# FFN blocks 4 to 10 with five steps by seven products, 9 of 27 sets of weight sums formed by VectorE, and a transpose in halves

## The chip, the cores and the metric

One of the cores of a Trainium2 chip runs one program. The metric is the device time of one execution in microseconds (us), as the median of several runs. A profile belongs to one execution of its own: its span goes from the first to the last instruction, and that execution's time is a little longer than the span.

Names used below: PE is the matrix engine (TensorE), DVE the vector engine, ACT the scalar engine, POOL is GpSimd, SP is the engine that issues most of the DMAs. SBUF is the on-chip memory, PSUM the accumulators of PE. Each engine takes its instructions strictly in program order, and an instruction that waits holds up everything behind it on that engine.

## The reference, cut to what matters

The program computes one decoder layer for 256 positions and a model width of 2048. The change touches the feed-forward network and the preparation of its weights:

```python
a = rmsnorm(h, norm_ffn_pre[layer])
gt, up = jnp.split(a @ w_ffn_gate_up[layer], [D_FF], axis=-1)    # D_FF = 5632
ff = (jax.nn.silu(gt) * up) @ w_ffn_down[layer]
h = h + rmsnorm(ff, norm_ffn_post[layer])
```

Ahead of it stand the big projection of the input (`a @ w_in`, 17408 columns), attention in three dilated groups, a gated recurrence, two branch projections and the mixing projection. Everything is float32, and the kernel keeps that precision by splitting.

## The kernel before

**Splitting.** Each float32 operand is split into a high part (rounded to the type that PE multiplies) and a low part (what is left). ACT writes the high part and DVE subtracts it from the original for the low part. A product is then three matmuls: high by high, high by low, low by high.

**Steps.** The weights are streamed once. A *step* takes 256 rows of a weight matrix by 1024 columns (two groups of 512), 1 MB, into one of three `raw` tiles of SBUF. ACT writes the high part `w` (three tiles, line 441 or 434), DVE the low part `wl` (line 456 or 436), and PE multiplies both with the 256 positions. In blocks: 2 halves of the rows, 2 halves of the columns, 2 halves of the positions give 8 block products and thus 24 matmuls of 128x128 by 512 columns. A *step by seven* does the same with 7 block products, after Strassen and Winograd, thus 21 matmuls. It needs four sums of the activation's blocks (`h7[m]`, made once for each pair of rows m by `pair_sums`) and four sums of the weight's blocks. Of these, one takes the place of the first quarter of `raw`, three stand in a tile `sum` of 1536 columns, which is split too: high part `dh` (ACT, line 454), low part `dl` (DVE, line 458). `dh` and `dl` share four tiles, that is two steps.

**Where the weight sums come from.** The list of a block's steps, for instance `GATE_UP4`, holds pairs (m, s). With s = 0 the step is plain. With s = 1 DVE forms the sums when the step is split (three additions, lines 445 to 451). With s = 2 they lie ready in device memory as `presum`, formed long before, and `fetch_sums` brings 768 KB of them to SBUF and `load_wide` the remaining quarter. The step's ordinary load is unchanged in size.

**Forming `presum`.** `weight_sums` is a generator of GpSimd DMAs that copy and add up within device memory, 8 DMAs of 256 KB for each set. `ahead_of_time(i)` advances it once at the end of an item, after a tiny copy on POOL (line 344, `beats`) that waits until the load three items ahead has landed. Before, there are 20 sets, two for each of the FFN blocks 1 to 10.

**Items.** The program is one list of items, worked off by a loop at the end of the kernel. Items 0 to 79 are ten blocks of eight steps of the big projection; 80 to 175 are its query and key columns in smaller *chunks*; 176 to 191 are gate columns; 192 to 207 the recurrence's branch, 208 to 223 the attention's branch (four blocks of four chunks, each chunk 12 matmuls); 224 to 239 the mixing; then come eleven FFN blocks of eight steps, and 44 steps of the down projection. Attention and recurrence run as generators (`lanes`), advanced once an item.

At item i the code first splits item i + 2 (`split`: a high part on ACT, a low part on DVE, and by seven also `dh` and `dl`), then issues the DMAs of `fetch_sums` for item i + 4 and of the load that is three raw tiles ahead, then multiplies item i, then advances what finishes earlier blocks, then `ahead_of_time`. That is the order on every engine. Since there are three `w` tiles, the high part of item i + 2 can be written only when PE has done with item i - 1.

**Finishing an FFN block.** `evac_ffn` adds up the four accumulators with DVE (line 537) and applies silu with ACT (line 1461); a product (line 1463), two casts (line 1414), four DMA transposes issued by SP (line 1420), two more casts (line 1429) and a store issued by ACT (line 1431) turn the result for the down projection. All of it happens during the first half of the next block.

**Memory phases.** At item 210 (`make_room`, called with c = 2 in the first block of the attention's branch) the tiles of the attention phase are closed.

**Planes.** `turned_inputs` brings gate and query inputs of the recurrence back from device memory with four DMA transposes (`planes`) in items 72 to 75.

Of the kernel before, what the change touches and what calls it, by code (L numbers as in the profile page):

```python
# [43 lines left out]
]  # L44
GATE_UP3 = [(3, 0), (4, 0), (0, 2), (5, 0), (1, 1), (6, 0), (2, 2), (7, 0)]
GATE_UP4 = [(4, 0), (5, 0), (0, 2), (6, 0), (1, 1), (2, 2), (3, 1), (7, 0)]
DOWN = [[(m, m in by7) for m in range(KF // 2)] for by7 in (range(4, 20, 3), (2, 4, 7, 10, 13, 16, 18))]

SPARSE = 128
N_F, N_RAW, N_SPLIT, AHEAD, WARM, BRIDGE = 17, 3, 3, 2, 8, 6  # L50


# [49 lines left out]
def tile_hybrid_block(ctx: ExitStack, tc: tile.TileContext, t, out):  # L102
# [194 lines left out]
    def weight_sums(jobs):  # L297
# [25 lines left out]
        for at in range(len(jobs) + 3):  # L323
# [5 lines left out]
            yield  # L329
            yield  # L330

    def fetch_sums(i):
        if i < len(items) and items[i][0] is steps:
            n = items[i][1]
            if n in pre:
                pre_in[n] = sum_slot()
                nc.sync.dma_start(pre_in[n], pre[n][:, 512:])

    def ahead_of_time(i):

        kind, n = items[i][:2]
        if back and (kind is steps or n >= SPARSE or n % 3):
            ahead = items[i + 3][0][items[i + 3][1]][2]
            nc.gpsimd.tensor_copy(beats, ahead[:, 1023:1024])  # L344
            advance(back)
# [213 lines left out]
    def pair_sums(src, out, slot, pairs=H7):  # L559

        for m in pairs:
            f = ptile("f").rearrange("p (k t) -> p k t", k=2)
            x = src.slots[m]
            nc.vector.tensor_add(f, x[:, :, 0, :].bitcast(F32), x[:, :, 1, :].bitcast(F32))
            dst = slot().rearrange("p (z n t) -> p z n t", z=2, n=4)
            yield
            for part in seven_sums(f, dst):
                yield
                part()
            out[m] = sums_of(dst)  # L570
            yield
# [95 lines left out]
        return row[:, None, :].to_broadcast([P, n, S])  # L667

    evacs, turns, lanes, queue = deque(), deque(), [deque(), deque()], deque()
    back, turned, hold, gathers = deque(), deque(), [False], []  # L670
    ready = set()

    def advance(q):
# [7 lines left out]
    def flush(q):  # L681
        while q:
            advance(q)
# [111 lines left out]
    def turned_inputs():  # L795

        planes = {}
        for half, name in product(range(2), "fq"):
            planes[name, half] = rslot("planes").bitcast(U16)
            nc.sync.dma_start_transpose(  # L800
                planes[name, half].rearrange("p (n t) -> p n t", n=8), waits[name, half]
            )
            yield
        nc.sync.dma_start(lmask, t["lmask"])

        def join(copy, name, half, z):
# [569 lines left out]
    def more_h(c):  # L1376
        if c + 1 < KD // 2:
            transpose_in(h_t, colg[:, 16:32], hT[0], c + 1)
        if c == 3:
            mix_gain(3, 1, wides[last_mix])  # L1380
            residual_of(6, (0, 1), False)
            residual_of(7, (0, 1), False)
            lanes[0].append(second_norm())
        if c == 4:
            lanes[1].append(pair_sums(hT[0], h7, lambda: rslot("so"), range(4)))

    def second_norm():
        ss, s2 = small("ss"), small("s2")
# [202 lines left out]
    def make_room(c):  # L1591
        if c == 2:
            flush(evacs)
            end_phase1()

    early = [
# [47 lines left out]
    add_wide_block(w, (0, FF), PLAIN, lambda k: hT[0](k), None, evac_first, True, mid=more_h)  # L1644
    spare = wides[-1], 0
    for j in range(1, 11):
        add_wide_block(w, (512 * j, FF + 512 * j), GATE_UP4 if j > 1 else GATE_UP3, lambda k: hT[0](k),
                       lambda m: h7[m], evac_ffn, j % 2 == 0,
                       pre=begin_wides if j == 1 else None, turn=1)
    for j in range(2):  # L1650
# [3 lines left out]

    wides[len(early) - 1].pre = lambda: turned.append(turned_inputs())
    wides[-3].post = lambda c: fetch_act(c // 2) if c in (1, 3) else None
    back.append(
        weight_sums([n for n, (b, i, *_) in enumerate(steps) if b.order[i][1] == 2])
    )

    load_x(0, 0, 256)
    load_wide(0, ((0, (0,)), (0, (1,))))
# [111 lines left out]
```

## Time and profile before

| what | value |
|---|---|
| runs of the kernel before | 1681.19, 1682.56 and 1685.92 us, median 1682.56 us |
| the profiled execution | 1683.17 us; its span is 1681.3 us, so 1.87 us lie around the span |
| DVE in the FFN blocks, busy in each 50 us from 1100 to 1400 us | 43.4 to 45.3 us |
| DMA in the same stretch | busy 0.85 to 0.95, 261 to 290 GB/s |
| DVE from 650 to 850 us | 26.5 to 33.3 us of each 50 us |
| DMA queues over the whole span | 423.47 MB, a mean of 252 GB/s |

How to read the page: the first row says how long each engine was busy. A PE that is busy all the time need not be at its peak, because a matmul's end is modelled, so the distance between the starts of matmuls is the better measure. The chain of work that ended last says which engine's work fills the span. The timeline shows start, duration and, in square brackets, how long the engine had been idle and what ended the wait. A busy engine costs nothing as long as PE does not wait for it.

### The profile page before, as it was taken

The numbers are of one execution on the slowest core, as the hardware profiler recorded it, in microseconds if no ns is written. First come the engines' busy times: TensorE is split into PE (matmuls) and PEld (weight loads), VectorE is DVE, ScalarE is ACT, GpSimd is POOL, SyncE is SP. The second block draws the span as 40 slices with busy tenths as digits, with TensorE's granted clock in tenths as the row PEclk, the third lists the DMA queues.
The fourth block names the chain that finished last, engine by engine and source line by source line (L and its number), as shares of the span: only waits on it lengthen the run. The fifth ranks groups of instructions, "written<-read, shape, count | busy, mean of one in ns | idle before, by whom it ended". The sixth has DMA issues, their size and how long they took to land.

```text
span 1681.3 us, 21780 instructions
## 1 busy us (share of the span) xinstructions
PE 1668.5 (99%) x8023; PEld 1397.5 (83%) x8023; DVE 1374.6 (82%) x1433; ACT 1001.3 (60%) x1077; POOL 238.0 (14%) x358
## 2 busy tenths in 40 slices
PE   9999999999999999999999999999999999999997
PEld 7888888888888888888888888888888888888886
DVE  6988888888796786674568978899888888998987
ACT  6667555555555555555545547666666666665653
POOL 0012333232352221222230100000000000000000
PEclk9999999999999999999999999999999999999999
DMA  8678999999988887778899746999888989987773
GB/s 279 216 250 263 288 275 279 276 284 261 280 232 236 256 232 184 195 226 265 254 222 308 227 173 201 283 275 289 268 267 273 271 271 277 274 282 261 240 266 114
DMA packets 258284, 423.47 MB, mean 252 GB/s; under 512 B 46801, under 2 KB 97153, under 8 KB 258177
## 3 DMA queue, kind: packets, MB, share of 16 engines
q1 hardware_dynamic: 231728, 360.83, 67.5%
q0 software_dynamic: 17984, 41.97, 12.5%
q10 hardware_dynamic: 8464, 19.28, 3.4%
q8 instruction: 63, 1.03, 0.3%
q14 instruction: 45, 0.36, 0.1%
HBM read 397.89 MB, written 58.20 MB: 271 GB/s over the span
## 4 chain that ended last, share of the span: by engine, by line
PE 98%; DVE 1%; ACT 1%; issue 0%; DVEq 0%; ACTq 0%
PE acc L139 59%; PE aux L139 37%; PE aux L991 0%; PE aux L632 0%; DVE fz L1552 0%; DVE wl L436 0%; ACT junk L1506 0%; PE aux L619 0%; DVE e L537 0%; DVE w L382 0%; ACT w L381 0%; ACT w L434 0%; PE aux L1187 0%; PE aux L1294 0%; DVE yT L600 0%
## 5 line engine op out<-in xcount | busy, mean ns | idle before, releaser
L436 DVE TENSOR_TENSOR wl<-raw,w 128x2048 fp32r<-128x2048 f32 (+1 forms) x150 | 327.3, 2189 | 79.9 <-ACT w L434 77.7
L434 ACT ACTIVATE w<-raw 128x2048 fp32r<-128x2048 f32 (+1 forms) x150 | 273.7, 1833 | 120.3 <-PE aux L139 33.8
L382 DVE TENSOR_TENSOR w<-raw,w 128x1024 fp32r<-128x1024 f32 x144 | 176.4, 1225 | 129.4 <-ACT w L381 129.3
L139 PE MATMUL acc<-xT,w 128*128 128x512 f32 (+1 forms) x1536 | 275.6, 338 | 0.0
L139 PEld LDWEIGHTS acc<-xT,w 128*128 128x128 f32 x1536 | 233.9, 188 | 33.9 <-DVE w L382 0.7
L381 ACT ACTIVATE w<-raw 128x1024 fp32r<-128x1024 f32 x144 | 152.0, 1058 | 153.4 <-PE acc L139 114.3
L344 POOL COPY beats<-raw 128x1 f32<-128x1 f32 x185 | 129.7, 701 | 746.1 <-DMA raw<-in_w_in 563.4
L456 DVE TENSOR_TENSOR wl<-raw,w 128x2048 fp32r<-128x2048 f32 x83 | 190.1, 2290 | 32.0 <-ACT w L441 16.5
L139 PE MATMUL acc<-w,xT 128*128 128x512 f32 x694 | 207.1, 391 | 0.0
L139 PE MATMUL acc<-w,hT 128*128 128x512 f32 x510 | 166.7, 391 | 0.4 <-DVE hT L1306 0.4
L444 ACT ACTIVATE w<-raw 128x1536 fp32r<-128x1536 f32 x63 | 93.9, 1491 | 111.1 <-PE acc L139 33.9
L139 PEld LDWEIGHTS acc<-w,xT 128*128 128x128 f32 x694 | 129.9, 188 | 26.8
L458 DVE TENSOR_TENSOR dl<-sum,dh 128x1536 fp32r<-128x1536 f32 x83 | 145.5, 1753 | 3.0 <-ACT dh L454 3.0
L139 PE MATMUL aux<-w,xT 128*128 128x512 f32 x454 | 145.0, 389 | 0.0
L139 PE MATMUL aux<-w,hT 128*128 128x512 f32 x414 | 134.6, 389 | 0.0
L454 ACT ACTIVATE dh<-sum 128x1536 fp32r<-128x1536 f32 x83 | 123.3, 1485 | 12.2 <-PE aux L139 4.1
L139 PEld LDWEIGHTS acc<-w,hT 128*128 128x128 f32 x510 | 95.7, 188 | 20.5 <-DVE hT L1306 0.9
L139 PEld LDWEIGHTS aux<-w,xT 128*128 128x128 f32 x454 | 85.2, 188 | 17.7
L139 PE MATMUL acc<-wl,hT 128*128 128x512 f32 x255 | 99.2, 389 | 0.0
L139 PE MATMUL acc<-wl,xT 128*128 128x512 f32 x251 | 97.7, 389 | 0.0
L139 PEld LDWEIGHTS aux<-w,hT 128*128 128x128 f32 x414 | 77.7, 188 | 16.1
L139 PE MATMUL aux<-w,a 128*128 128x512 f32 x282 | 89.1, 389 | 0.0
(282 smaller groups left out, 3032.8 us busy)
## 6 DMA issues: line engine op xcount, KB each, us to landing
raw<-in_w_in SPq DMA_DIRECT2D x270, 512.0 KB, 6.1
raw<-in_w_ffn_gate_up SPq DMA_DIRECT2D x156, 512.0 KB, 5.4
raw<-in_w_ffn_down SPq DMA_DIRECT2D x88, 512.0 KB, 5.6
presum<-in_w_ffn_gate_up POOLq DMA_DIRECT2D x120, 256.0 KB, 6.5
raw<-in_w_mix_out SPq DMA_DIRECT2D x32, 512.0 KB, 5.1
sum<-presum SPq DMA_DIRECT2D x20, 768.0 KB, 6.7
act<-acts SPq DMA_DIRECT2D x22, 512.0 KB, 6.8
presum<-presum POOLq DMA_DIRECT2D x40, 256.0 KB, 6.4
```

The lines of the kernel that those rows point to most:

```text
L139: nc.tensor.matmul(ps, lhsT, rhs, start=start, stop=stop, skip_group_check=True)
L344: nc.gpsimd.tensor_copy(beats, ahead[:, 1023:1024])
L381: nc.scalar.activation(wh, raw, AF.Copy)
L382: nc.vector.tensor_sub(wl, raw, wh.bitcast(F32))
L434: nc.scalar.activation(hi[:, c], raw[:, c], AF.Copy)
L436: nc.vector.tensor_sub(lo[:, c], raw[:, c], hi[:, c].bitcast(F32))
L444: nc.scalar.activation(hi[:, 512:], raw[:, 512:], AF.Copy)
L454: nc.scalar.activation(high, sums, AF.Copy)
L456: nc.vector.tensor_sub(lo, raw, hi.bitcast(F32))
L458: nc.vector.tensor_sub(low, sums, high.bitcast(F32))
```

## The change

- **Five steps by seven.** A new list `GATE_UP5` is used for FFN blocks 4 to 10 in place of `GATE_UP4`. Position for position the kinds of steps are the same but at the fourth place of eight, where a plain step becomes one with s = 2. Block 1 keeps `GATE_UP3`, blocks 2 and 3 keep `GATE_UP4`. For the fifth pair of rows `pair_sums` makes `h7[4]`, after a pause of eight advances.
- **27 sets.** Blocks 1 to 3 have two sets each, blocks 4 to 10 three. 18 of them (blocks 1 to 6 and 10) come from `weight_sums` as before.
- **Nine sets by DVE.** Those of blocks 7 to 9 are made by a new generator, `weight_sums_beside`: SP loads four quarters of 256 KB into two tiles, three items later DVE adds (two additions, then one and one in the next items), one item later ACT issues two stores of 512 KB. One such set takes nine items. Two of these generators run from items 166 and 181 on, and `make_room` runs what is left of them to its end at item 210.
- **Pacing of `weight_sums`.** Up to chunk 95 it now advances in seven items of eight (before: two of three), from chunk 96 to 137 not at all, and not in wide block 9 (items 72 to 79).
- **Planes in halves.** Eight DMA transposes of half the size, one an item, in place of four.

```diff
--- before.py
+++ after.py
@@ -44,9 +44,10 @@
 ]
 GATE_UP3 = [(3, 0), (4, 0), (0, 2), (5, 0), (1, 1), (6, 0), (2, 2), (7, 0)]
 GATE_UP4 = [(4, 0), (5, 0), (0, 2), (6, 0), (1, 1), (2, 2), (3, 1), (7, 0)]
+GATE_UP5 = [(5, 0), (6, 0), (0, 2), (2, 2), (1, 1), (4, 2), (3, 1), (7, 0)]
 DOWN = [[(m, m in by7) for m in range(KF // 2)] for by7 in (range(4, 20, 3), (2, 4, 7, 10, 13, 16, 18))]
 
-SPARSE = 128
+PAUSE, QUIET, BESIDE = (96, 138), 9, (166, 181)
 N_F, N_RAW, N_SPLIT, AHEAD, WARM, BRIDGE = 17, 3, 3, 2, 8, 6
 
 
@@ -329,6 +330,28 @@
             yield
             yield
 
+    def weight_sums_beside(jobs):
+
+        for n in jobs:
+            x = [fslot("pre") for _ in range(2)]
+            b, i = steps[n][:2]
+            m = b.order[i][0]
+            r = [x[g][:, c * 512 : (c + 1) * 512] for g, c in ((0, 1), (0, 0), (1, 0), (1, 1))]
+            for q, (g, k) in enumerate(product(range(2), repeat=2)):
+                rows = slice((2 * m + k) * P, (2 * m + k + 1) * P)
+                nc.sync.dma_start(r[q], b.w[rows, b.cols[g] : b.cols[g] + 512])
+            for _ in range(3):
+                yield
+            for to, by in ((2, 0), (0, 1), (1, 2), (3, 1)):
+                nc.vector.tensor_add(r[to], r[to], r[by])
+                if by:
+                    yield
+            pre[n] = dram.tile([P, 2048], F32, name=nm("presum"))
+            for g in range(2):
+                nc.scalar.dma_start(pre[n][:, g * 1024 : (g + 1) * 1024], x[g])
+            for _ in range(3):
+                yield
+
     def fetch_sums(i):
         if i < len(items) and items[i][0] is steps:
             n = items[i][1]
@@ -338,8 +361,15 @@
 
     def ahead_of_time(i):
 
+        for n, q in enumerate(beside):
+            if i >= BESIDE[n]:
+                advance(q)
         kind, n = items[i][:2]
-        if back and (kind is steps or n >= SPARSE or n % 3):
+        if kind is chunks:
+            parts = n % 8 > 0 if n < PAUSE[0] else n >= PAUSE[1]
+        else:
+            parts = n // 8 != QUIET
+        if back and parts:
             ahead = items[i + 3][0][items[i + 3][1]][2]
             nc.gpsimd.tensor_copy(beats, ahead[:, 1023:1024])
             advance(back)
@@ -559,6 +589,8 @@
     def pair_sums(src, out, slot, pairs=H7):
 
         for m in pairs:
+            for _ in range(8 if m == 4 else 0):
+                yield
             f = ptile("f").rearrange("p (k t) -> p k t", k=2)
             x = src.slots[m]
             nc.vector.tensor_add(f, x[:, :, 0, :].bitcast(F32), x[:, :, 1, :].bitcast(F32))
@@ -667,7 +699,7 @@
         return row[:, None, :].to_broadcast([P, n, S])
 
     evacs, turns, lanes, queue = deque(), deque(), [deque(), deque()], deque()
-    back, turned, hold, gathers = deque(), deque(), [False], []
+    back, beside, turned, hold, gathers = deque(), (deque(), deque()), deque(), [False], []
     ready = set()
 
     def advance(q):
@@ -797,10 +829,13 @@
         planes = {}
         for half, name in product(range(2), "fq"):
             planes[name, half] = rslot("planes").bitcast(U16)
-            nc.sync.dma_start_transpose(
-                planes[name, half].rearrange("p (n t) -> p n t", n=8), waits[name, half]
-            )
-            yield
+            for z in range(2):
+                c = slice(z * 512, (z + 1) * 512)
+                nc.sync.dma_start_transpose(
+                    planes[name, half][:, z * 1024 : (z + 1) * 1024].rearrange("p (n t) -> p n t", n=4),
+                    waits[name, half][:, c],
+                )
+                yield
         nc.sync.dma_start(lmask, t["lmask"])
 
         def join(copy, name, half, z):
@@ -1382,7 +1417,7 @@
             residual_of(7, (0, 1), False)
             lanes[0].append(second_norm())
         if c == 4:
-            lanes[1].append(pair_sums(hT[0], h7, lambda: rslot("so"), range(4)))
+            lanes[1].append(pair_sums(hT[0], h7, lambda: rslot("so"), range(5)))
 
     def second_norm():
         ss, s2 = small("ss"), small("s2")
@@ -1591,6 +1626,8 @@
     def make_room(c):
         if c == 2:
             flush(evacs)
+            for q in beside:
+                flush(q)
             end_phase1()
 
     early = [
@@ -1644,7 +1681,7 @@
     add_wide_block(w, (0, FF), PLAIN, lambda k: hT[0](k), None, evac_first, True, mid=more_h)
     spare = wides[-1], 0
     for j in range(1, 11):
-        add_wide_block(w, (512 * j, FF + 512 * j), GATE_UP4 if j > 1 else GATE_UP3, lambda k: hT[0](k),
+        add_wide_block(w, (512 * j, FF + 512 * j), (None, GATE_UP3, GATE_UP4, GATE_UP4)[j] if j < 4 else GATE_UP5, lambda k: hT[0](k),
                        lambda m: h7[m], evac_ffn, j % 2 == 0,
                        pre=begin_wides if j == 1 else None, turn=1)
     for j in range(2):
@@ -1654,9 +1691,10 @@
 
     wides[len(early) - 1].pre = lambda: turned.append(turned_inputs())
     wides[-3].post = lambda c: fetch_act(c // 2) if c in (1, 3) else None
-    back.append(
-        weight_sums([n for n, (b, i, *_) in enumerate(steps) if b.order[i][1] == 2])
-    )
+    kept = [n for n, (b, i, *_) in enumerate(steps) if b.order[i][1] == 2]
+    back.append(weight_sums(kept[:15] + kept[24:]))
+    for n, q in enumerate(beside):
+        q.append(weight_sums_beside(kept[15:24][5 * n : 5 * n + 5]))
 
     load_x(0, 0, 256)
     load_wide(0, ((0, (0,)), (0, (1,))))
```

Two places show how the instructions move. The first is on DVE in an FFN block from the fourth on: the low part of the third step (`wl`, `dl`), the product that finishes the block before (`e`), and the next two or three steps. Before:

```order
L456 TENSOR_TENSOR wl_10188<-raw_10090,w_10187 128x2048
L458 TENSOR_TENSOR dl_10191<-sum_10119,dh_10190 128x1536
L1463 TENSOR_TENSOR e_10136<-e_10136 128x1024
L436 TENSOR_TENSOR wl_10229<-raw_10121,w_10228 128x2048
L445 TENSOR_TENSOR sum_10269<-raw_10154 128x1024
L450 TENSOR_TENSOR raw_10154<-raw_10154,sum_10269 128x512
```

The same place of the changed kernel, whose lines in the file have moved down by 30 to 35:

```order
L486 TENSOR_TENSOR wl_10296<-raw_10195,w_10295 128x2048
L488 TENSOR_TENSOR dl_10299<-sum_10224,dh_10298 128x1536
L1498 TENSOR_TENSOR e_10242<-e_10242 128x1024
L486 TENSOR_TENSOR wl_10337<-raw_10226,w_10336 128x2048
L488 TENSOR_TENSOR dl_10340<-sum_10260,dh_10339 128x1536
L475 TENSOR_TENSOR sum_10381<-raw_10262 128x1024
L480 TENSOR_TENSOR raw_10262<-raw_10262,sum_10381 128x512
```

One `dl` has come in; on ACT one `dh` comes in at the same place, and on SP two more DMAs (the quarter of `presum` and 768 KB of `sum`). Nothing else moves in these blocks.

The second place is item 210, where `make_room` ends the two new generators. On SP, loads of the attention's branch (`raw`) and the four quarters of the ninth set (`pre`) stand like this in the changed kernel:

```order
L272 DMA raw_7253<-in_w_attn_branch 128x2x512 x2
L272 DMA raw_7292<-in_w_attn_branch 128x2x512 x2
L342 DMA pre_7314<-in_w_ffn_gate_up 128x512 x2
L342 DMA pre_7315<-in_w_ffn_gate_up 128x512 x2
L272 DMA raw_7339<-in_w_attn_branch 128x2x512 x2
```

The load `raw_7292` takes the tile of `raw_7145`, whose last reader is the low part `w_7320` of item 211. On DVE, the low parts of items 210 to 214 (`w`), before:

```order
L382 TENSOR_TENSOR w_7203<-raw_7069,w_7203 128x1024
L1214 TENSOR_TENSOR part_7223<-acc_7122,gate_6846 128x512
L382 TENSOR_TENSOR w_7227<-raw_7069,w_7227 128x1024
L1214 TENSOR_TENSOR part_7223<-acc_7123,gate_6846 128x512
L382 TENSOR_TENSOR w_7245<-raw_7119,w_7245 128x1024
L382 TENSOR_TENSOR w_7270<-raw_7119,w_7270 128x1024
L382 TENSOR_TENSOR w_7289<-raw_7167,w_7289 128x1024
```

and in the changed kernel:

```order
L412 TENSOR_TENSOR w_7320<-raw_7145,w_7320 128x1024
L1249 TENSOR_TENSOR part_7309<-acc_7205,gate_6916 128x512
L412 TENSOR_TENSOR w_7336<-raw_7201,w_7336 128x1024
L346 TENSOR_TENSOR pre_7315<-pre_7315,pre_7314 128x512
L346 TENSOR_TENSOR pre_7314<-pre_7314 128x512
L346 TENSOR_TENSOR pre_7314<-pre_7314,pre_7315 128x512
L346 TENSOR_TENSOR pre_7315<-pre_7315,pre_7314 128x512
L412 TENSOR_TENSOR w_7366<-raw_7201,w_7366 128x1024
```

The four additions of the last set stand directly between the low parts of items 212 and 213, one low part behind the one that frees the tile for `raw_7292`. On ACT the two stores of that set stand between the high parts of items 212 and 213:

```order
L411 ACTIVATE w_7336<-raw_7201 128x1024
L351 DMA presum_7358<-pre_7314 128x1024
L351 DMA presum_7358<-pre_7315 128x1024
L411 ACTIVATE w_7366<-raw_7201 128x1024
L411 ACTIVATE w_7381<-raw_7253 128x1024
```

The eight other sets have their additions spread over three items, and their stores stand one item behind the last addition.

## The prediction

> **What bounds the kernel now.** I read the page first, then the waits of PE, the chain of waits, and then one FFN block on each engine.
>
> ```profile
> span 1681.3 us, 21780 instructions
> ...
> PE 1668.5 (99%) x8023; PEld 1397.5 (83%) x8023; DVE 1374.6 (82%) x1433; ACT 1001.3 (60%) x1077; POOL 238.0 (14%) x358
> ...
> PE 98%; DVE 1%; ACT 1%; issue 0%; DVEq 0%; ACTq 0%
> ```
>
> PE fills the span and the chain. Since a busy PE need not be at its peak, I look at whom it waited for, and at how fast its matmuls follow each other.
>
> ```profile
> PE aux L632 <- DVE wl L392: 1.3, 1, 1.3
> PE aux L139 <- DVE warm L163: 1.2, 1, 1.2
> PE acc L139 <- DVE hT L1306: 0.4, 1, 0.4
> PE acc L139 <- DVE gate L1224: 0.2, 1, 0.2
> PE aux L991 <- DVE p L985: 0.2, 1, 0.2
> ```
>
> Those are all waits of PE in the whole execution: 2.5 us at the start and 0.8 us later. So nothing that only removes waits can win even a microsecond; a gain must come from fewer matmuls.
>
> ```profile
> 1196.49 11.56 PE aux L139 x51
> ...
> 1237.29 11.56 PE acc L139 x51
> 1252.25 6.80 PE acc L139 x30
> ```
>
> In the chain, 51 matmuls take 11.56 us and 30 take 6.80 us: 0.2267 us each. The same place of the next FFN block comes 40.80 us later, which is 180 matmuls (4 plain steps of 24, 4 by seven of 21) at 0.2267 us, without a gap. A plain step takes 5.44 us, one by seven 4.76 us.
>
> **The change part by part.** *Matmuls.* In blocks 4 to 10 one plain step becomes one by seven: 7 x 3 = 21 matmuls less, 21 x 0.2267 = **-4.76 us**. A block then takes 177 x 0.2267 = 40.12 us, if DVE, ACT and the DMAs keep up.
>
> *DVE in these blocks.* Each gets one more `dl`.
>
> ```profile
> 1196.55:1237.35 40.80, 40.80 (x181) 33.78 (x180) 36.06 (x27) 27.23 (x22) 0.00 (x0) 1.00 0.87 268
> ```
>
> ```profile
> 1213.33 2.29 DVE L456 TENSOR_TENSOR wl<-raw,w 128x2048 fp32r<-128x2048 f32 x1
> 1215.53 1.75 DVE L458 TENSOR_TENSOR dl<-sum,dh 128x1536 fp32r<-128x1536 f32 x1
> 1217.20 1.22 DVE L445 TENSOR_TENSOR sum<-raw 128x1024 f32<-128x1024 f32 x1
> 1218.45 0.69 DVE L450 TENSOR_TENSOR raw<-raw,sum 128x512 f32<-128x512 f32 x1
> 1219.18 0.69 DVE L451 TENSOR_TENSOR sum<-raw 128x512 f32<-128x512 f32 x1
> ...
> 1234.85 1.88 DVE L537 TENSOR_TENSOR e<-aux,e 128x512 f32<-128x512 f32 x3
> 1237.33 0.69 DVE L537 TENSOR_TENSOR e<-aux,e 128x512 f32<-128x512 f32 x1 [0.60 <-PE aux L139]
> 1239.33 2.29 DVE L456 TENSOR_TENSOR wl<-raw,w 128x2048 fp32r<-128x2048 f32 x1 [1.31 <-ACT w L441]
> ```
>
> DVE is busy for 36.06 us of a block and idle for 4.74. With 1.75 us for `dl` it needs 37.8 of 40.12 us, so at most 2.3 us of waiting may be left. Which waits stay when DVE runs late? Those for PE go, since PE is then ahead. One stays: after the third L537 ends at 1236.73, ACT has still to do a silu and the next high part before DVE can start the `wl` of 1239.33; these 2.60 us hold only one more L537 of 0.69, so 1.9 us are idle whatever the lag. 37.8 + 1.9 = 39.7 us against 40.12: it fits, by 0.4 us. I cost DVE at nothing here, with little cover; its price without cover is a rival below.
>
> *ACT in these blocks.* One more `dh` of 1.49 us, in a queue that is busy for 27.2 of 40.8 us.
>
> ```profile
> 1215.18 2.60 ACT L1429 ACTIVATE act<-e 128x1024 uint16<-128x1024 uint16 x2 [1.20 <-DMA e<-e]
> 1217.81 0.33 ACTq L1431 DMA_DIRECT2D acts<-act  x1
> 1218.24 1.49 ACT L444 ACTIVATE w<-raw 128x1536 fp32r<-128x1536 f32 x1 [0.46 <-ACT act L1429]
> 1219.63 0.61 ACT L452 ACTIVATE w<-raw 128x512 fp32r<-128x512 f32 x1
> 1222.14 1.49 ACT L454 ACTIVATE dh<-sum 128x1536 fp32r<-128x1536 f32 x1 [1.90 <-PE aux L139]
> ```
>
> The last row shows a `dh` that waits for PE to leave the step that last used its tile. With five steps by seven in a row this wait comes earlier: the sixth step's `dh` waits for the fourth step's end, 2 x 5.44 + 2 x 4.76 = 20.40 us into the block. Behind it on ACT stand the casts, the store and the seventh step's high part, and behind that DVE's `wl`: 1.49 + 2.60 + 0.33 + 1.49 + 0.61 + 2.29 = 8.8 us, so 29.2. PE wants that low part in the second matmul of the seventh step, at 20.40 + 2 x 4.76 + 0.23 = 30.15. So **1.0 us of slack** remains at the tightest place. The casts wait for four transposes; behind a `dh` of 1.49 us they start at about 18.6 + 1.5 = 20.1 us into the block (18.63 is 1215.18 less 1196.55), before 21.9, when that `dh` ends, so they stay hidden.
>
> *DMAs in these blocks.* 768 KB more in each.
>
> ```profile
> sum<-presum SPq DMA_DIRECT2D x20, 768.0 KB, 6.7
> ...
> 1230.00:1240.00 10.00, 10.00 (x46) 8.28 (x45) 7.89 (x9) 5.73 (x5) 0.00 (x0) 1.00 0.99 360
> ```
>
> 268 GB/s over 40.8 us are 10.9 MB; with 0.79 MB more in 40.12 us it is 292 GB/s, while a busy 10 us moves 360. A sum is issued some 10 us before its `dh` and lands in 6.7. Nothing, with a rival for the other case.
>
> *The nine sets of DVE.* 36 additions of 0.69 us (L450's shape) are 25 us, 18 stores at 0.33 us (L1431) are 6 us of ACT.
>
> ```profile
> 690.00:912.00 222.00, 221.62 (x1155) 188.28 (x1154) 144.36 (x208) 117.56 (x154) 51.16 (x93) 1.00 0.85 241
> ```
>
> There DVE idles for 78 us and ACT for 104. For eight sets the additions come two or three items behind the loads' issue; an item of 3.6 us or so makes that 7 to 11 us, and a late one delays low parts with two items of room. Between 0 and 2 us; I take 0.3, near the row.
>
> *The ninth set* is the exception. Item 210 ends it at once.
>
> ```profile
> 856.01 1.23 DVE L382 TENSOR_TENSOR w<-raw,w 128x1024 fp32r<-128x1024 f32 x1 [0.89 <-ACT w L381]
> ...
> 858.73 1.23 DVE L382 TENSOR_TENSOR w<-raw,w 128x1024 fp32r<-128x1024 f32 x1 [0.89 <-ACT w L381]
> ...
> 865.80 1.07 ACT L381 ACTIVATE w<-raw 128x1024 fp32r<-128x1024 f32 x1 [1.66 <-PE acc L139]
> ...
> 1200.85 0.34 SPq L284 DMA_DIRECT2D raw<-presum  x1
> ...
> 1206.29 0.89 SPq L290 DMA_DIRECT2D raw<-in_w_ffn_gate_up  x2
> ...
> raw<-in_w_ffn_gate_up SPq DMA_DIRECT2D x20, 256.0 KB, 4.4
> ...
> presum<-in_w_ffn_gate_up POOLq DMA_DIRECT2D x120, 256.0 KB, 6.5
> ...
> DMA to landing us min/median/max: 3.0/5.6/9.3
> ```
>
> Item 211's low part (the row at 856.01; in the order, the one between the two `part` rows) ends at 857.24 and frees the tile for SP's next load. SP then issues two loads (0.89) and four quarters (0.34 each), the third quarter at 858.8, the fourth at 859.2. Taking 5.0 us to landing, between 4.4 and 6.5, the third, which the first addition needs, lands at 863.8. Only then do the four additions run, in steps of 0.73 (1218.45 to 1219.18): 866.7. Behind them ACT issues two stores (0.67) and only then writes item 213's high part (1.06), and DVE the low part (1.23): 869.7. PE wants it at 865.8: the row at 865.80 is released by the end of item 212. **+3.8 us**, with nothing behind to hide it, since PE has no gap. With 3.0 us to landing it is 1.8, with 9.3 it is 8.1.
>
> [...]
>
> *The rest.* Two sets less on POOL, other pacing, planes in halves, `h7[4]` (some 2.7 us of DVE in block 2, beside 4.7 idle): PE waits for none of their sources in the rows of waits, so they win nothing; a loss is bounded by the 0.2 us waits there. Nothing.
>
> *Sum*: -4.76 + 3.8 + 0.3 = -0.7 us. The profiled execution took 1683.17 us (span 1681.3 and 1.87 around it), 0.6 above the median of 1682.56, so the forecast on the median's scale is **1681.9 us**.
>
> **The rivals.** (1) *No stall at item 210.* Then -4.76 + 0.3: 1678.1 us. Against it stands that the third quarter would have to land within about 1 us. For it: PE may be late there for other reasons, or SP may issue earlier than I read.
>
> (2) *DVE sets the pace* (slower than before). If each DVE instruction started only when the one ahead has ended, the 0.09 us that now overlap (2.29 long, next start after 2.20) at some 20 seams a block, about 1 us in all with the smaller ones, would have to be paid whenever DVE is late: 38.8 + 1.9 = 40.7 us a block. It decides from 40.12 on. Seven blocks lose 7 x 0.58 = 4.1, less the slack of 1.0: 3.1, with the stall at item 210 a sum of +2.4: 1685.0 us. The rows speak against it, as the overlap is there when DVE runs without a wait. [...] Worse, if all 4.74 us of idle time stayed, a block would take 42.5 us: 7 x 2.4 - 1.0 = 15.8 more, 1697.7 us.
>
> (3) *Late transfers in the FFN blocks.* Landings up to 9.3 us are seen; if the added 0.79 MB made one step of each block late by 0.5 to 1 us: +3.5 to 7, 1685 to 1689 us.
>
> (4) *The additions hurt attention*, which PE follows closely (the 0.2 us wait on `p`): +2 to 4, 1684 to 1686 us.
>
> **How the numbers follow.** Forecast (stall at item 210, blocks otherwise at PE's pace) 0.60, own range 1679.9 to 1686.2 by the landing of 3.0 to 9.3 us; rival 1 0.14; rival 2 0.09, its worse form 0.03; rival 3 0.08; rival 4 0.06. From 1677.8 (rival 1 less 0.3) to 1686.5 (the forecast's slow end, rival 2 and parts of 3 and 4) more than 8 in 10 are held. A measurement of this kernel tells about 0.3%, 5 us, from no change. The matmuls can win 4.76 at most, so faster than that takes rival 1 and a favourable measurement: 0.06. Slower by 5 us (above 1687.6) are rival 2's worse form and a part of rival 3: 0.07. The rest is 0.87.
>
> **What would show it.** Blocks 4 to 10 at 40.12 us between like places in the chain, with DVE idle for about 2.3 us in each: the matmul term. A wait of PE near the first block of the attention's branch for the low part or high part of a chunk, 2 to 5 us long, with DVE's first `pre` addition waiting for a DMA just ahead: the stall. Blocks longer than 40.2 us with PE waiting for `wl` would show rival 2, for a `raw` behind ACT rival 3. My forecast is wrong if no wait of PE over 1 us shows between 850 and 880 us, or if PE waits more than 1 us in sum within the FFN blocks.

## The result and the profile after

The changed kernel takes a median of 1706.04 us (1704.31 to 1711.03), beside 1683.86 us (1681.19 to 1685.92) for the kernel before in the same comparison: a ratio of 1.0141, with a 95% interval of 1.0129 to 1.0154. It is 22.2 us slower, where the prediction had 0.7 less and a range up to 1686.5. The profiled execution took 1704.31 us, with a span of 1702.5, which is 21.2 more than before.

First the page of the changed kernel: span, busy times, and the shares of the chain of work that ended last.

```profile
span 1702.5 us, 21844 instructions
...
PE 1672.0 (98%) x8002; PEld 1397.9 (82%) x8002; DVE 1407.6 (83%) x1482; ACT 1010.7 (59%) x1085; POOL 213.1 (13%) x326
...
PE 87%; DMA 5%; DVE 4%; ACT 2%; issue 1%; SPq 1%; POOL 0%; ACTq 0%; DVEq 0%; POOLq 0%
```

PE had 98% of the chain before; now DMA, DVE and ACT have 11% between them. Then the waits of PE in the changed kernel (total us, times, longest):

```profile
PE acc L140 <- ACT w L411: 6.9, 2, 6.0
PE acc L140 <- DVE w L412: 6.7, 4, 4.3
PE aux L1026 <- DVE m L1019: 2.3, 1, 2.3
PE aux L1026 <- DVE p L1020: 1.6, 2, 1.4
```

These four rows, 17.5 us, are new but for 0.2 on `p`; the others are those of before, with 0.8 us for the first `x` in place of 1.3 for `wl` at the start and 0.5 more for `gate`. L411 and L412 write the high and the low part of a chunk, and L1019 and L1020 belong to attention, so it is the stretch of the chunks and of attention that suffers. The table by stages shows where (busy us of PE, PEld, DVE, ACT, POOL with their counts, then the granted clock, the DMA share and GB/s):

```profile
700.00:750.00 50.00, 44.14 (x253) 38.15 (x252) 29.93 (x48) 22.98 (x35) 11.36 (x24) 0.93 0.80 235
750.00:800.00 50.00, 50.00 (x259) 42.62 (x258) 29.88 (x44) 24.58 (x32) 0.00 (x0) 1.00 0.85 294
800.00:850.00 50.00, 46.36 (x228) 38.61 (x227) 34.07 (x56) 25.17 (x36) 0.00 (x0) 0.97 0.91 318
850.00:900.00 50.00, 43.49 (x197) 35.54 (x196) 31.08 (x38) 15.78 (x19) 1.03 (x2) 0.93 0.77 262
...
1221.34:1261.46 40.12, 40.12 (x178) 33.22 (x178) 37.34 (x28) 28.56 (x22) 0.00 (x0) 1.00 0.93 294
```

Three stretches of 50 us lose 16.0 us of PE's busy time, and in the same three the granted clock falls to 0.93, 0.97 and 0.93, which at these rounded digits is some 8 us more. With the waits of 1.7 us at 581 (below) that is about 26, and 21.2 plus the 4.76 us won by the matmuls is 26.0. The last row is one FFN block: exactly as long as predicted, and PE never idle.

Whom does DVE wait for between 690 and 930 us? This is its longest entry there, and then SP's longest between 700 and 890:

```profile
DVE pre L346 <- DMA pre<-in_w_ffn_gate_up: 35.6, 7, 9.7
```

```profile
SPq L272 <- DVE w L412: 105.6, 22, 16.4
```

The first addition of seven of the nine sets finds its quarter not yet there. The second row is what the prediction reckoned with for the ninth set alone and overlooked for the other eight: SP's ordinary loads wait for DVE's low parts, which free the raw tiles, and the quarters are queued behind those loads. Two sets on SP and on DVE, the first one and the ninth (start, duration, in brackets the idle time before and what ended it):

```profile
721.32 0.92 SPq L272 DMA_DIRECT2D raw<-in_w_in  x2
722.28 2.26 SPq L342 DMA_DIRECT2D pre<-in_w_ffn_gate_up  x4
...
873.94 2.02 SPq L342 DMA_DIRECT2D pre<-in_w_ffn_gate_up  x4
```

```profile
720.04 1.22 DVE L412 TENSOR_TENSOR w<-raw,w 128x1024 fp32r<-128x1024 f32 x1
721.17 0.69 DVE L975 TENSOR_TENSOR qk<-sum,w 128x512 f32<-128x512 f32 x1
721.84 1.23 DVE L412 TENSOR_TENSOR w<-raw,w 128x1024 fp32r<-128x1024 f32 x1
722.98 0.75 DVE L244 TENSOR_TENSOR sum<-acc,sum 128x256 f32<-128x256 f32 x2
724.62 1.23 DVE L412 TENSOR_TENSOR w<-raw,w 128x1024 fp32r<-128x1024 f32 x1 [0.89 <-ACT w L411]
735.51 0.69 DVE L346 TENSOR_TENSOR pre<-pre,pre 128x512 f32<-128x512 f32 x1 [9.67 <-DMA pre<-in_w_ffn_gate_up]
...
874.46 1.23 DVE L412 TENSOR_TENSOR w<-raw,w 128x1024 fp32r<-128x1024 f32 x1 [0.89 <-ACT w L411]
883.02 0.69 DVE L346 TENSOR_TENSOR pre<-pre,pre 128x512 f32<-128x512 f32 x1 [7.34 <-DMA pre<-in_w_ffn_gate_up]
```

DVE's low part ends at 721.26, SP's waiting load goes out at 721.32 and the quarters from 722.28 on. DVE has only two low parts left before it is at the addition, at 725.85: 3.6 us after the first quarter was issued. For the ninth set it is 1.8 us (873.94 to 875.69). How long a quarter takes from its issue to its landing (least, median, most):

```profile
DMA to landing us min/median/max: 4.9/8.2/13.1
```

So DVE stands still for 9.7, 8.3 and 7.3 us at three of the sets, and for 0.7 to 4.0 us at four others. Since it works in order, the next low part stands behind the addition: at the first set ACT has written its high part at 727.42 us (1.06 from 726.36 on), and DVE starts it at 736.85, behind two additions. PE's rows at the ninth set:

```profile
874.71 6.73 PE L140 MATMUL acc<-w,attnT 128*128 128x512 f32 x29
887.49 0.80 PE L140 MATMUL acc<-w,attnT 128*128 128x512 f32 x1 [6.05 <-ACT w L411]
888.75 6.58 PE L140 MATMUL acc<-w,attnT 128*128 128x512 f32 x19 [0.46 <-DVE w L412]
```

After the stop, 19 matmuls take 6.58 us, where at 0.2267 they would take 4.31. The stop itself lasts 7.3 us (from 881.44 to 888.75, with a single matmul in it), and the slow matmuls behind it cost 2.3 more.

### The profile page after: what moved, and what is told of

The parts are those of the page before. It is cut to its first block, busy times and chain, and to the rows that moved or that the text cites. A ratio compares the mean times of both kernels' runs of the same rounds, so it can differ in the third digit from the quotient of the medians.

```text
span 1702.5 us, 21844 instructions
## 1 busy us (share of the span) xinstructions
PE 1672.0 (98%) x8002; PEld 1397.9 (82%) x8002; DVE 1407.6 (83%) x1482; ACT 1010.7 (59%) x1085; POOL 213.1 (13%) x326
## 4 chain that ended last, share of the span: by engine, by line
PE 87%; DMA 5%; DVE 4%; ACT 2%; issue 1%; SPq 1%; POOL 0%; ACTq 0%; DVEq 0%; POOLq 0%
PE acc L140 52%; PE aux L140 34%; DMA pre<-in_w_ffn_gate_up 2%; DMA raw<-in_w_in 2%; DVE w L412 1%; DMA raw<-in_w_mix_out 1%; ACT w L411 1%; DVE wl L466 1%; ACT w L464 1%; PE aux L1026 0%; DVE pre L346 0%; DMA x<-in_x 0%; DVE fz L1587 0%; PE aux L664 0%; DMA e<-e 0%
## 5 line engine op out<-in xcount | busy, mean ns | idle before, releaser
L466 DVE TENSOR_TENSOR wl<-raw,w 128x2048 fp32r<-128x2048 f32 (+1 forms) x143 | 311.2, 2183 | 75.0 <-ACT w L464 74.3
L464 ACT ACTIVATE w<-raw 128x2048 fp32r<-128x2048 f32 (+1 forms) x143 | 260.2, 1828 | 113.0 <-PE aux L140 33.0
L412 DVE TENSOR_TENSOR w<-raw,w 128x1024 fp32r<-128x1024 f32 x144 | 176.1, 1224 | 99.6 <-ACT w L411 99.6
L411 ACT ACTIVATE w<-raw 128x1024 fp32r<-128x1024 f32 x144 | 151.6, 1057 | 165.2 <-PE acc L140 101.3
L486 DVE TENSOR_TENSOR wl<-raw,w 128x2048 fp32r<-128x2048 f32 x90 | 206.1, 2290 | 26.3 <-ACT w L471 20.8
L374 POOL COPY beats<-raw 128x1 f32<-128x1 f32 x169 | 114.3, 676 | 818.2 <-DMA raw<-in_w_in 535.4
L488 DVE TENSOR_TENSOR dl<-sum,dh 128x1536 fp32r<-128x1536 f32 x90 | 157.7, 1752 | 0.7 <-ACT dh L484 0.7
L140 PE MATMUL acc<-w,hT 128*128 128x512 f32 x460 | 152.5, 391 | 0.4 <-DVE hT L1341 0.4
L484 ACT ACTIVATE dh<-sum 128x1536 fp32r<-128x1536 f32 x90 | 133.7, 1485 | 13.9 <-PE acc L140 5.0
L140 PEld LDWEIGHTS acc<-w,hT 128*128 128x128 f32 x460 | 86.3, 188 | 18.6 <-DVE hT L1341 0.9
L140 PE MATMUL acc<-wl,hT 128*128 128x512 f32 x230 | 89.5, 389 | 0.0
L140 PE MATMUL aux<-wl,xT 128*128 128x512 f32 x227 | 88.3, 389 | 0.0
```

What stands on the lines that cost most here:

```text
L140: nc.tensor.matmul(ps, lhsT, rhs, start=start, stop=stop, skip_group_check=True)
L411: nc.scalar.activation(wh, raw, AF.Copy)
L412: nc.vector.tensor_sub(wl, raw, wh.bitcast(F32))
L464: nc.scalar.activation(hi[:, c], raw[:, c], AF.Copy)
L466: nc.vector.tensor_sub(lo[:, c], raw[:, c], hi[:, c].bitcast(F32))
L484: nc.scalar.activation(high, sums, AF.Copy)
```

## The experiments

Theory 1 is what the traces above suggest: the quarters land later than DVE comes to them, DVE waits in order, the low parts are late. Its rivals: the 25 us of additions are the cost themselves (rival 2), or the added transfers make ordinary loads late (rival 3). In this section the rivals have these numbers; they are not those of the prediction. The kernel before ran beside each group, with medians of 1683.86 us (the changed kernel), 1682.14 (the next four rows), 1682.33 (the four behind them) and 1682.05 (the last four); the ratios are to it.

| kernel | median us | ratio, 95% interval |
|---|---|---|
| changed | 1706.04 | 1.0129 to 1.0154 |
| 27 sets on POOL | 1690.89 | 1.0037 to 1.0067 |
| nine sets only | 1702.17 | 1.0103 to 1.0137 |
| gap of six items | 1693.79 | 1.0056 to 1.0095 |
| additions on POOL | 1688.13 | 1.0022 to 1.0048 |
| sums shared | 1678.58 | 0.9967 to 0.9985 |
| early, old pacing | 1686.22 | 1.0013 to 1.0031 |
| early, new pacing | 1680.03 | 0.9975 to 0.9993 |
| early, old pacing, halves | 1685.07 | 1.0006 to 1.0024 |
| early start alone | 1693.20 | 1.0049 to 1.0079 |
| pacing and planes alone | 1690.78 | 1.0042 to 1.0069 |
| early, quiet middle | 1677.56 | 0.9965 to 0.9985 |
| early, short | 1686.91 | 1.0010 to 1.0028 |

**The two halves of the change apart.** First five steps by seven with all sets on POOL, at the old pacing:

```diff
-    back.append(weight_sums(kept[:15] + kept[24:]))
-    for n, q in enumerate(beside):
-        q.append(weight_sums_beside(kept[15:24][5 * n : 5 * n + 5]))
+    back.append(weight_sums(kept))
```

> The five steps by seven alone: all 27 sets are made by POOL's adding transfers at the old pacing, the planes are whole again, and DVE and SP have nothing of the nine sets. Theory 1 (quarters of the nine sets land 8 to 12 us after their issue, DVE waits for them in order, the low parts behind are late, and PE's clock falls after each stop) and rival 2 (the 25 us of additions on DVE are the cost themselves) both expect the matmul term alone: 1679 us, 4 to 5 below the kernel before, at most 2 us more if the later transfers of POOL disturb the branches. If the FFN blocks were the place of the loss (prediction's rivals 2 and 3), this stays at 1700 or above.

It took 1690.89 us: a miss for both theories. The reason is the experiment's own. With 27 sets POOL is not done before the FFN blocks. One stretch there, and ACT's wait for raw tiles between 1000 and 1300 us:

```profile
1150.00:1200.00 50.00, 45.31 (x191) 36.23 (x191) 42.50 (x30) 35.54 (x28) 16.89 (x19) 0.97 1.05 319
```

```profile
ACT w L460 <- DMA raw<-in_w_ffn_gate_up: 32.5, 10, 6.6
```

POOL is still busy with sets there, the DMA share is over 1, and loads are late (in the changed kernel ACT waits 9.8 us for them in the same window). The changed kernel has no such stop, so this does not explain it. The other half:

```diff
-    back.append(weight_sums(kept))
+    back.append(weight_sums(kept[:9] + kept[18:]))
+    for n, q in enumerate(beside):
+        q.append(weight_sums_beside(kept[9:18][5 * n : 5 * n + 5]))
```

> The nine sets alone: the kernel before, with its lists, pacing and whole planes, but nine of its 20 sets (half of block 5, blocks 6 to 9) are made beside by SP, DVE and ACT at the same items as in the changed kernel. Theory 1 and rivals 2 (DVE's own time) and 3 (the traffic starves ordinary loads) expect most of the changed kernel's loss and the lost matmul gain on top: 1684 + 20 to 25 = 1704 to 1709 us. If the loss comes from five by seven, or only from it together with the sets, it is 1684 to 1688.

1702.17 us, 20.0 above its own kernel before, the lower end of the 20 to 25 expected: the nine sets alone bring most of the loss, and DVE waits 29.6 us for quarters. To have the first half clean, the nine sets were then left out altogether:

```diff
-    for n, q in enumerate(beside):
-        q.append(weight_sums_beside(kept[15:24][5 * n : 5 * n + 5]))
+    like.update(zip(kept[15:24], kept[6:15]))
...
-            if n in pre:
+            if like.get(n, n) in pre:
```

> Five steps by seven without the making of nine sets: blocks 7 to 9 read the sums of nine sets that POOL makes anyway for blocks 4 to 6 (so these nine sets of sums are left out of the computation), with the old pacing and whole planes; the FFN blocks execute the same instructions and transfers as in the changed kernel. Theory 1: the FFN blocks are sound and worth the matmul term, 4.76 us, with nothing to pay: 1678 to 1679.5 us, no wait of PE over 1 us behind 120 us. The rival from the run with 27 sets on POOL, whose FFN blocks lost 8 us to late loads: if the 5th step's own transfers are what makes loads late there, waits for low parts stand between 1090 and 1280 us here too, and the time is 1684 to 1690.

1678.58 us, 3.75 below the kernel before. The FFN blocks are sound, as expected: no wait of PE stands in them. Against the expectation PE stops once elsewhere, for 2.1 us near 418 us in the big projection; the cause of that stays open. That the gain is 1.0 us less than the matmul term lies within the interval (0.9967 is 5.6 us, 0.9985 is 2.5).

**More time between loads and additions.**

```diff
-            for _ in range(3):
+            for _ in range(6):
                 yield
             for to, by in ((2, 0), (0, 1), (1, 2), (3, 1)):
...
-            for _ in range(3):
-                yield
```

> The changed kernel with six items instead of three between a set's loads and its first addition, and none behind the stores, so that a set takes nine items as before; the ninth set, ended at item 210, stays as it is. Theory 1: a landing of 8 to 12 us is covered by six items of 3.6 us, so the stops near 733, 801 to 805 and 830 us go (about 12 us with the slow clock behind them) and the one near 881 stays (about 8): 1692 to 1696 us, and DVE's waits for the quarters fall from 35.6 us to 8 to 12. Rival 2 (the additions' own time) and rival 3 (traffic): 1703 to 1708, since the same additions and transfers remain.

1693.79 us. That is 11.7 above its own kernel before, where the changed kernel was 22.2 above its own: 10.5 us less, as theory 1 expected and neither rival did, since the additions and the transfers are the same. DVE's wait for quarters from 690 to 930 us, and PE's two longest kinds of waits in this run:

```profile
DVE pre L346 <- DMA pre<-in_w_ffn_gate_up: 9.3, 1, 9.3
```

```profile
PE acc L140 <- ACT w L409: 9.8, 2, 8.6
PE acc L140 <- DVE w L410: 1.2, 2, 0.8
```

One wait is left, the ninth set's, while a quarter still lands after a median of 7.6 us. Not the landing became shorter, but DVE comes later. The 10.5 us are what is left after the ninth set's stop grew (its longest wait is 8.6 us here and 6.0 in the changed kernel), and with such intervals they are known to some 4 us. Now the ninth set:

```diff
-PAUSE, QUIET, BESIDE = (96, 138), 9, (166, 181)
+PAUSE, QUIET, BESIDE = (96, 138), 9, (160, 175)
```

> The changed kernel, with its gap of three items, its pacing and its halves, but both generators started six items earlier (160 and 175), so that the ninth set is done before item 210 in the ordinary rhythm. Theory 1: the stop at the ninth set (6.2 us and the slow clock behind it, 9 to 10 us together) goes, the stops of the other sets stay, perhaps at other items: 1694 to 1698 us. If the ninth set only takes over a delay that the others hand down, little changes: 1702 or above.

1693.20 us, 11.2 above its own kernel before, so 11.0 less than the changed kernel, a little more than expected. DVE still waits 21.7 us for quarters, and PE stops near 718, 776 and 781 us, but no longer at the ninth set. The earlier start moves the other sets too (DVE's waits for their quarters were 28.3 us in the changed kernel), so the 11.0 us are not the ninth set's alone.

**The additions on POOL.**

```diff
-                nc.vector.tensor_add(r[to], r[to], r[by])
+                nc.gpsimd.tensor_add(r[to], r[to], r[by])
...
-                nc.scalar.dma_start(pre[n][:, g * 1024 : (g + 1) * 1024], x[g])
+                nc.gpsimd.dma_start(pre[n][:, g * 1024 : (g + 1) * 1024], x[g])
```

> The changed kernel with the 36 additions done by POOL and the 18 stores issued by POOL; SP's loads are the same. Theory 1: only POOL waits for the quarters, nothing of PE stands behind it, so all four stops of the attention stretch go, the ninth set's too: 1680 to 1684 us. Rival 2 expects the same. Rival 3 (the added transfers make raw tiles late): 1700 or above, with waits of ACT for raw where DVE waited for quarters. A POOL slower than DVE at additions could make its other work late: up to 1690.

1688.13 us, 4 above the range of theory 1 and below the 1690 left open for a slow POOL. The ninth set's stop is gone and DVE waits for no quarter, with the same loads and stores; that is against rival 3 here. What is left are the stop near 580 us (below), one of 2.3 us near 737, one of 0.9 near 765 and two of 1.8 near 908 and 920, about the start of the mixing. Ahead of the last, ACT takes 10.2 us to issue four loads (`hx`) that cost it 3.2 in the kernel before, and its next high part stands behind them; why they take so long is not shown:

```profile
900.00:950.00 50.00, 46.17 (x209) 37.41 (x208) 38.05 (x31) 25.81 (x20) 8.96 (x12) 1.00 0.91 292
```

```profile
906.04 10.16 ACTq L1281 DMA_DIRECT2D hx<-in_x  x4
916.25 1.92 ACT L464 ACTIVATE w<-raw 128x2048 fp32r<-128x2048 f32 x1 [9.63 <-DMA hx<-in_x]
```

**Both cures, and POOL's pacing.** With the gap of six and the early start, and whole planes, three kernels differ in POOL's pacing and in the planes:

```diff
-        if kind is chunks:
-            parts = n % 8 > 0 if n < PAUSE[0] else n >= PAUSE[1]
-        else:
-            parts = n // 8 != QUIET
-        if back and parts:
+        if back and (kind is steps or n >= 128 or n % 3):
```

> The changed kernel with the six-item gap, both generators started six items earlier (160 and 175), so that the ninth set's loads are issued at item 202 and its additions have eight items, and with the old pacing and whole planes. Theory 1: no addition waits for its quarters for more than a us or two, no stop of PE in the attention stretch, none at 580 us: 1678 to 1681 us, faster than before by 2 to 5. Rival 2 (36 additions of 0.69 us on DVE cost by themselves) and rival 3 (the 18.9 MB added there make raw tiles late): still 1690 or above.

> The same with the changed kernel's pacing of POOL and whole planes. Where the 2 us near 580 us come from POOL's denser transfers in the weight stage, they are here and the time is 2 us above the kernel with the old pacing, some 1 more near 915 us where POOL's last sets run: 1680 to 1684. Where they come from the planes in halves, there is no stop at 580: 1678 to 1681.

> The same with the old pacing and the planes in halves. Pacing as the cause: no stop near 580, 1678 to 1681 us. Planes as the cause: 1 to 2 us of PE waiting near 580 us, 1680 to 1683.

The old pacing gave 1686.22, the new 1680.03, the old with halves 1685.07 us. The new pacing was expected to be 2 us slower than the old one and is 6.2 faster. Here theory 1 alone is not enough: with the old pacing DVE hardly waits for quarters (2.2 us in all), and still those 6 us are lost. The stretch from 750 to 850 us, first with the old, then with the new pacing:

```profile
750.00:800.00 50.00, 47.48 (x232) 40.06 (x231) 29.37 (x44) 24.35 (x32) 7.62 (x16) 0.97 1.03 332
800.00:850.00 50.00, 46.34 (x234) 38.51 (x234) 33.26 (x51) 22.48 (x31) 6.61 (x12) 1.00 1.05 365
```

```profile
750.00:800.00 50.00, 48.48 (x245) 40.84 (x244) 35.95 (x55) 27.85 (x38) 0.00 (x0) 1.00 0.97 353
800.00:850.00 50.00, 50.00 (x263) 42.81 (x262) 35.75 (x54) 26.03 (x35) 0.00 (x0) 1.00 0.93 318
```

POOL's sets together with the nine sets bring the DMA share over 1, and with the old pacing ACT waits 11.6 us for loads of the recurrence's branch (1.6 with the new). That is rival 3, in a place where the changed kernel avoids it by its pause. In turn the new pacing has a stop of 2.3 us near 580 us, which both kernels with the old pacing lack. (Stops with no row beside them are counted by the starts of PE's matmuls, as the distance less the ordinary 0.2267 us; the rows of waits, which go by modelled ends, are some tenths shorter: 2.8 beside 2.95 in the run with the early start.) In the changed kernel PE's waits from 570 to 590 us are these:

```profile
PE acc L140 <- ACT w L411: 0.9, 1, 0.9
PE acc L140 <- DVE w L412: 0.8, 1, 0.8
```

Whole planes or halves make no difference that shows: 1686.22 and 1685.07 have overlapping intervals.

The pacing and the halves alone, on the kernel before:

> The new pacing and the planes in halves alone, on the kernel before with its 20 sets all on POOL and its lists. From the runs with the early nine sets: a stop of about 2.3 us near 580 us and at most 1 near the mixing, 1684 to 1686 us, while the pause cannot win anything here since no nine sets share its time. If the denser pacing needs the nine sets to do harm, 1682 to 1683. The 20 sets end later than before (in the FFN blocks 1 to 3), which might cost 1 to 3 more, as in the run with 27 sets.

1690.78 us, more than expected, even with the 1 to 3 us for late sets. The stop near 580 is there (2.3 us), and one of 3.6 us near 986 with a slow clock behind it (0.97 granted from 950 to 1000 us), where PE waits for DVE's `zg`; with 20 sets, many are left for the mixing (320 GB/s from 900 to 950 us), which fits this stop but does not show its cause. The changed kernel, with 18 sets on POOL, has no such stop there.

**Two attempts at the stop near 580.** Both start from the kernel with the early sets, the new pacing and whole planes.

```diff
-            parts = n % 8 > 0 if n < PAUSE[0] else n >= PAUSE[1]
+            parts = n % (3 if 40 <= n < 64 else 8) > 0 if n < PAUSE[0] else n >= PAUSE[1]
```

> The kernel with the early nine sets, six items of gap, whole planes and the new pacing, but POOL advances only in two items of three for chunks 40 to 63, around 580 us. Theory: the stop there (1.3 and 1.0 us) goes and all else stays: 1677 to 1679 us. If the stop belongs to the sets' count up to there rather than to the density just there, it stays or moves: 1680.

1677.56 us, faster than both kernels: 4.5 us below the kernel before, whose median in this group was 1682.05. All waits of PE in this run:

```profile
PE aux L140 <- DVE warm L164: 1.2, 1, 1.2
PE acc L140 <- DVE hT L1336: 0.4, 1, 0.4
PE acc L140 <- DVE gate L1254: 0.2, 1, 0.2
PE aux L1021 <- DVE p L1015: 0.2, 1, 0.2
```

None is left that the kernel before does not have, with all 36 additions on DVE. The other attempt:

```diff
-            parts = n % 8 > 0 if n < PAUSE[0] else n >= PAUSE[1]
+            parts = n % 3 > 0 if n < 80 else n >= PAUSE[1]
```

> The same with two items of three up to chunk 79 (the old pacing) and then the pause up to chunk 138. No stop near 580 us, as with the old pacing; the pause keeps 700 to 900 us free: 1677 to 1679 us. More sets are left for the mixing and the first FFN blocks (some 47 of 168 advances behind item 218), which by the run with 27 sets may cost up to 3 us there: then 1679 to 1682.

1686.91 us, a miss. The stop near 580 is gone, but the sets left over run in the mixing and the first FFN blocks, and PE waits 3.2 us for `zg` near 981. Its profiled execution took 1683.28 us, so the trace does not show all that the median lost.

## Why the prediction was wrong

**Right: the matmul term (-4.76).** The chain of the changed kernel has the same place of successive FFN blocks at these times:

```profile
1181.22 11.56 PE acc L140 x51
...
1221.34 11.56 PE aux L140 x51
...
1261.46 11.56 PE acc L140 x51
```

That is 40.12 us a block, the predicted figure to the last digit.

**Right: DVE, ACT and the DMAs in the blocks, at nothing.** In the block from 1221.34 us DVE is busy for 37.34 us (predicted 37.8), ACT for 28.56 (27.2 and a `dh` of 1.49), the DMAs move 294 GB/s (predicted 292), and PE is never idle. So the prediction's rival 2 falls in both forms, and its rival 3 did not occur in this kernel; what it describes was seen with 27 sets on POOL.

**Wrong: "the nine sets of DVE", taken as 0.3.** This is the step that failed. It gave the additions "7 to 11 us" behind the loads' issue by counting two or three items of 3.6 us. But the loads' issue hangs on DVE: SP waits for a low part to free a raw tile, and from that low part to the addition DVE had only two more to do at the first set. 3.6 us were left at the first set and 2.8 at the set issued at 788.83, and a quarter lands after a median of 8.2. Nor did the two items of room absorb the late low parts. The run with the larger gap puts the price at **10.5 us**, give or take 4. The prediction's rival 4 named the right stretch, with 2 to 4 us and for another reason: the additions themselves cost nothing that can be seen, as the kernel with the quiet middle shows, which has them all.

**Right in mechanism, wrong in size: the ninth set, taken as 3.8.** Every link of it is in the trace: SP issues the quarters behind the waiting load, DVE waits, ACT's two stores go ahead of the high part, PE stops. But the quarters landed some 8 us after their issue instead of the assumed 5.0. With 7.9 in place of 5.0 the prediction's own terms (which add up to 3.9, not 3.8) give 6.8; the stop became 7.3 us, and the clock added 2.3, **9.6 us** in all by this trace. The run with the early start is 11.0 us shorter, but it moves the other sets too. The rows that gave 4.4 and 6.5 as the bounds were of other stretches, without nine sets in flight.

**Missing: the clock.** No term priced what follows a stop. The rows at 888.75 us show it: 2.3 us behind a stop of 7.3, with a granted clock of 0.50 from 889 to 892.7 us. By the table of stages it is some 8 of the 26 us lost.

**Wrong: "the rest", taken as nothing.** The prediction bounded this loss by the rows of waits of the kernel before, which do not tell what denser transfers do. POOL's denser pacing brings a stop of about 2 us near 580 us; every run with it has one there, and none of those with two items of three at that place. From 580 to 590 us PE is busy for 8.12 us in the early run with the new pacing and for all 10.00 in the one with the old.

Both cures together (with whole planes) took the changed kernel from 22.2 above to 2.3 below the kernel before, which is 24.5 us. That is 3.0 more than the two one by one, less than the intervals can tell from nothing. What is left, 2.3 us of gain, is close to the matmul term and the stop near 580 us: -4.76 + 2.3 = -2.5. With the 24.5 the sum is 22.0, beside 22.2 measured, but the 24.5 are themselves taken from the 22.2, so that only the -2.5 is tested here.

Two things stay open. Why a quarter lands so late was not taken apart by a run (the queue behind raw loads, POOL's transfers beside it, or the ACT queue's stores); it lands as late in kernels without a stop, after a median of 7.9 us in the one with the quiet middle. The trace narrows it down: from 873.9 to 883.0 us, on the ninth set's way, SP's queue moved 2.48 MB, of which the four quarters are 1.05, ACT's stores 0.52 and POOL's queue nothing, while from 721.3 to 735.5, on the first set's, POOL's queue moved 1.16 of 3.49 MB. And the stop near 580 was cured by thinning POOL's work around it, but what exactly its loads collide with there stays open.

## What to carry to other kernels

Where an engine waits in order for a load, count the time from the load's issue to the wait in the trace, not in items of the program: if the load is queued behind another that waits for this same engine, the distance shrinks to the few instructions between, here to 3.6 and 2.8 us where 7 to 11 had been counted. The new side work was cheap once the engine that it borrows hardly had to wait for it (DVE waited 35.6 us for quarters in the changed kernel, 1.5 in the early run with the new pacing): six items instead of three and an earlier start turned 22.2 us of loss into 2.3 of gain with the same additions and, but for whole planes, the same transfers, and thinner work for POOL at one place made it 4.5. And price a stop of PE with the slow matmuls behind it, which were 2.3 us behind the ninth set's 7.3.

## What the chip showed that was not expected

After some stops the matmuls run slow for a while. Behind the ninth set's stop of 7.3 us in the changed kernel, the starts of matmuls of 512 columns stand 0.427 us apart instead of 0.2267, eight times in a row from 889.34 to 892.75 us, and the granted clock is 0.50 from 889 to 892.7. It is 0.50 too behind the stop of 4.4 us (738 to 742.7) and behind one of 2.4 us (807.7 to 811). With the stop of 3.6 us near 986 in the run of pacing and planes alone, and with PE's wait of 3.2 us near 981 in the early run with the short stretch, it is 0.97 over the 50 us from 950 on. The expectation for 27 sets on POOL has the clock fall after each stop; it does not. One of 2.95 us in the run with the early start and one of 2.7 in the one with the old pacing left it as it was (1.00 from 700 to 750 and from 800 to 850 us), and so did the pair of 1.3 and 1.0 us near 580 in the early run with the new pacing (1.00 from 580 to 590). Why some stops are followed by slow matmuls and others not stays open.

The DMA share alone is no sure warning. Three stretches of 50 us with 1.03 to 1.05 (319 to 365 GB/s; the early run with the old pacing, and 27 sets on POOL) lost 2.5 to 4.7 us of PE, but one with 1.06 and 312 GB/s in the run with 27 sets (1200 to 1250 us) lost none, nor did one with 1.09 and 281 GB/s in the kernel before (400 to 450 us).
